# Block products for the down projection of a hybrid layer's second FFN

## The chip, the cores and the metric

One core of one Trainium2 chip runs the whole layer in one launch. The metric is the device time of that launch in microseconds (us). TensorE (PE in the profile) multiplies 128x128 blocks into PSUM, VectorE (DVE) and ScalarE (ACT) do the elementwise work, GpSimd (POOL) does some of it and issues transfers, SyncE (SP) issues transfers.

## The reference

The layer has three sub-layers, each with an RMSNorm before it and one after it: a SwiGLU feed-forward network (FFN), a mixer (a gated linear recurrence beside windowed attention), and a second FFN. There are 512 tokens, a model width of 1024 and an FFN width of 2816, that is 22 chunks of 128. All data is float32. The change lies in the second FFN:

```python
def swiglu(x, w_gu, w_down):
    gate, up = jnp.split(x @ w_gu, 2, axis=-1)
    return (jax.nn.silu(gate) * up) @ w_down
...
        x = x + 0.5 * rms_norm(swiglu(rms_norm(x, ffn2_pre_g[l]), ffn2_w_gu[l], ffn2_w_down[l]), ffn2_post_g[l])
```

## The kernel before

**Three terms for one product.** Each float32 operand is split into a high part, rounded to `float32r` by an ACT copy, and a low part, the difference, taken by DVE. A product of two blocks is three matmuls into one PSUM bank: high by high, high by low, low by high.

**Units of weights.** The class `Weights` keeps the order of all weight work. A raw tile of 1 MB comes from HBM on SP's queue into one of `NRAW` = 3 buffers. A unit is 128x1024 numbers of it: an optional sum of raw blocks on DVE (`pre`, L220), a cast to the high part on ACT (L171, L211), and the low part on DVE (L176, L215). `take()` hands the next unit to TensorE and brings the preparation up to four units beyond it (`AHEAD`). `later(n, ...)` puts a step n units later. So nothing is scheduled by a compiler: each engine runs its instructions in the order in which the program wrote them, and waits on semaphores.

**Gate and up product.** From chunk 6 on (chunk 4 in the first FFN), `quad` makes two chunks of the hidden layer by seven block products instead of eight: a unit is 24 matmuls of 128x256 into one of three banks A, D and B (names `ab`, `db`, `bb` in the second FFN, L676). Its end gives `u2` and `g1`, the hidden values of the first and of the second half of the tokens. `low_parts` splits them into high and low (L680 on ACT, L683 on DVE), in pieces of 128x256.

**Down product.** The 22 chunks of the second FFN go in five groups, `GROUPS2` = 0-6, 6-10, 10-14, 14-18 and 18-22. Group 0 uses plain products. Groups 1 to 3, here called the middle groups, run two quads and then, for each half `dh` of the output's columns, 4 chunks by 4 token blocks by three matmuls of 128x512 (`mm3_out`, L1425 to L1427, into four banks `yb`). The eight blocks of the running sum `yp_b`, 128x512 each, are kept in SBUF: ACT copies them there after group 0, DVE adds each middle group's banks to them (L1446). The last group adds its product, squares, scales by the norm, turns the residual stream `xT` back by transposes (`otp`, L1481), adds it and stores the result (L1488 to L1512). `xT`, eight tiles of 128x512, stays in SBUF from the start of the kernel.

Of the kernel before, what the change touches and what calls it, by code (L numbers as in the profile page):

```python
# [15 lines left out]
P = 128  # L16
T = 512
# [11 lines left out]
NT2K = 44  # L29
NW = 8  # L30
NWS = 6
NRAW = 3
CLASSIC1, CLASSIC2 = 4, 6
PUMPS = [(2, 1)] * 8 + [(1, 1), (1, 0), (4, 0)]
FILLS = {1: 4, 2: 5, 4: 5, 5: 5, 7: 5}
WARM = 6
# [12 lines left out]
class Weights:  # L49
# [18 lines left out]
    def load(self):  # L68
# [43 lines left out]
def tile_layer(ctx: ExitStack, tc: tile.TileContext, out: bass.AP, **ins: bass.AP):  # L112
# [6 lines left out]
    tmp = ctx.enter_context(tc.tile_pool(name="tmp", bufs=2))  # L119
    small = ctx.enter_context(tc.tile_pool(name="small", bufs=4))  # L120
    psum = ctx.enter_context(tc.tile_pool(name="psum", bufs=8, space=bass.MemoryType.PSUM))
    E = mybir.EngineType
    ctx.enter_context(tc.manual_schedule(engines={E.PE, E.DVE, E.Activation, E.Pool, E.SP}))

    ALL = slice(0, T)
    HALF = [slice(0, T // 2), slice(T // 2, T)]

    def bank(name):
# [12 lines left out]
    def load_raw(srcs, nk, w, name):  # L141
        raw = wpool.tile([P, nk * w], F32, tag="raw", name=f"raw_{name}", bufs=NRAW).rearrange("p (k c) -> p k c", k=nk)
        o = 0
        for src in srcs:
            n = src.shape[1]
            sync.dma_start(raw[:, :, o:o + n], src.rearrange("(k p) c -> p k c", p=P))
            o += n
        return raw

    class Deferred:  # L150
# [5 lines left out]
        def run(self):  # L156
            dve.tensor_sub(*self.args)
# [110 lines left out]
    def add_down(f, n, dh):  # L268

        r = W.raw(lambda: load_raw([ins["ffn2_w_down"][0, f * P:(f + n) * P, dh * T:(dh + 1) * T]], n, T, f"bd{f}{dh}"))  # L270
        for i in range(0, n, 2):
            add_unit(r, lambda raw, i=i: raw[:, i:i + 2, :], 2, T, f"bd{f + i}{dh}")

    for f0, f1 in GROUPS2:
        for f in range(f0, f1, 2):
            (add_gate_up if f < CLASSIC2 else add_quad)(w2, f, "b")
        if f1 < FC:
# [58 lines left out]
    def preload(func):  # L336
        act.activation(dummy, eps, func)
# [84 lines left out]
            return o  # L422


    xT = [big.tile([P, T], F32, name=f"xT{c}", tag=f"xT{c}") for c in range(KD)]

    def x_parts(name):
        return [(t2k(f"xh_{name}{c}", F32R), t2k(f"xl_{name}{c}", F32R)) for c in range(KD)]
# [7 lines left out]
    class Next:  # L436
# [14 lines left out]
        def low(self, c, h):  # L451
            x_low(self.xs[c], xT[c][:, HALF[h]], col(self.pre, c), HALF[h])

# [184 lines left out]
    class Hidden:  # L638
# [21 lines left out]
            dve.tensor_sub(hl, us, hh.bitcast(F32))  # L660
            self.hs[f] = (hh, hl)

        def quad(self, f, last, ahead):

            n = f"{self.name}{f}"
            l, r = HALF
            hs = [(t2k(f"hh{n}{j}", F32R), t2k(f"hl{n}{j}", F32R)) for j in range(2)]

            def seven(b, form, first, ahead=AHEAD):
                hi, lo = W.take(ahead)  # L670
                for j in range(2):
                    o, js = b[:, HALF[j]], slice(j * P, (j + 1) * P)
                    for k in range(4):
                        xh, xl = self.nxt.t[form, k]
                        for i, (w, x) in enumerate(((hi, xh), (hi, xl), (lo, xh))):
                            pe.matmul(o, w[:, k, js], x, start=first and i + j + k == 0, stop=k == 3 and i == 2, skip_group_check=True)  # L676

            def low_parts(x, h):
                for j in range(2):
                    act.copy(hs[j][0][:, HALF[h]], x[:, HALF[j]])  # L680
                for j in range(2):
                    hh, hl = hs[j]
                    dve.tensor_sub(hl[:, HALF[h]], x[:, HALF[j]], hh.bitcast(F32)[:, HALF[h]])  # L683

            def last_half():
                dve.tensor_mul(g1, g1, u4)

            A, D, B = (bank(f"{s}{n}") for s in "adb")
            p1, p7, u2, u4, g1 = (wt(f"{s}{n}") for s in ("p1", "p7", "u2", "u4", "g1"))
            seven(A, "b11", True)  # L690
            act.copy(p1, A)
            seven(D, "t3", True)
            act.copy(p7, D)
            seven(A, "t2", False)
            act.copy(u2, A)
            seven(B, "b21", True)
            dve.tensor_add(p1, p1, B)  # L697
            W.later(1, act.activation, p1, p1, AF.Silu)
            seven(A, "t1", False)
            act.copy(u4, A)  # L700
# [6 lines left out]
            act.activation(g1, A, AF.Silu)  # L707
# [6 lines left out]
            for j in range(2):  # L714
                self.hs[f + j] = hs[j]

        def classic(self, n, banks, extra, ahead=AHEAD):

# [32 lines left out]
        def chunks(self, f0, f1, ahead=AHEAD):  # L751
            for f in range(f0, f1, 2):
                self.quad(f, f == f1 - 2, ahead if f == f1 - 2 else AHEAD)
            return [self.hs.pop(f) for f in range(f0, f1)]


    n1 = Next("a", gain=lambda c: g1[:, c:c + 1])
# [668 lines left out]
        pe.matmul(ps, hh[:, blk], lo[:, k, cs], start=False, stop=False)  # L1426
        pe.matmul(ps, hl_[:, blk], hi[:, k, cs], start=False, stop=stop)  # L1427

    parts = {}
    for g, (f0, f1) in enumerate(GROUPS2[:-1]):  # L1430
        hs = hid.chunks(f0, f1) if g else hid.classic(f1, banks, {3: [(n2.sums, 0)], 3.5: [(n2.lows, 0)], 4.5: [(n2.sums, 1)], 5: [(n2.lows, 1)]}, AHEAD - 1)
        for dh in range(2):
            ybanks = [bank(f"yb{g}{dh}{tb}") for tb in range(NB)]
            for f in range(f0, f1):
                if f % 2 == 0:
                    w = W.take()
                for tb in range(NB):
                    mm3_out(ybanks[tb], hs[f - f0], tb, w, f % 2, ALL, f == f0, f == f1 - 1)
                if g == 0 and (dh, f) in ((0, 0), (0, 2), (1, 2), (1, 4)):
                    (n2.sums if f == 2 * dh else n2.lows)(2 + dh)  # L1440
            for tb in range(NB):
                if g == 0:
                    parts[tb, dh] = t2k(f"yp_b{tb}{dh}")
                    act.copy(parts[tb, dh], ybanks[tb])
                else:
                    dve.tensor_add(parts[tb, dh], ybanks[tb], parts[tb, dh])  # L1446
    f0, f1 = GROUPS2[-1]
    hs = hid.chunks(f0, f1, ahead=5)
    preload(AF.Sqrt)
    grow = [t2k(f"grow{dh}") for dh in range(2)]  # L1450
    for dh in range(2):
# [12 lines left out]
    for tb in range(NB):  # L1464
# [7 lines left out]
        tot = small.tile([P, 1], F32, tag="tot", name=f"tot_b{tb}")  # L1472
        for i, f in steps:
            dh, c0, c1 = pieces[i]
            if (i, f) == (1, f0):

                tp = []
                for h in range(2):
                    tp.append(bank(f"otp{tb}{h}"))
                    for c in range(4):  # L1480
                        pe.transpose(tp[h][:, c * P:(c + 1) * P], xT[4 * h + c][:, tb * P:(tb + 1) * P], ident)  # L1481
                if end:
                    tail = wt("tail")[:, :T // 2]
                    act.copy(tail, tp[1][:, :T // 2])
            mm3_out(banks[i][:, :c1 - c0], hs[f - f0], tb, weights(f, dh), f % 2, slice(c0, c1), f == f0, f == f1 - 1)
            if f == f1 - 1:
                y = parts[tb, dh][:, c0:c1]
                dve.tensor_add(y, banks[i][:, :c1 - c0], y)  # L1488
                act.activation(wt(f"ysq{tb}{i}")[:, :c1 - c0], y, AF.Square, accum_out=ss[:, i:i + 1])  # L1489
                if end and i == 2:  # L1490
                    dve.tensor_add(tot, ss[:, 0:1], ss[:, 1:2])
                    last = wt("last")[:, :c1 - c0]
                    dve.tensor_mul(last, y, grow[dh][:, c0:c1])
                else:
                    pool.tensor_mul(y, y, grow[dh][:, c0:c1])  # L1495
# [45 lines left out]
```

## Time and profile before

| | |
|---|---|
| median of 3 runs | 884.54 us (884.53 to 886.26) |
| the profiled execution: its own time | 886.26 us |
| the profiled execution: span in the trace | 884.6 us |
| one middle group, from its first quad product to the next group's (the chain of waits) | 62.10 us |
| data moved by DMA | 86.68 MB |

The span runs from the first to the last instruction of the trace; the execution's own time is 1.66 us longer. The columns of the profile's lines are explained where they are first used. A matmul's duration in a row covers its way through the pipeline, so matmuls overlap, and the time that one of many takes is read from when the next starts.

### The profile page before, as it was taken

To read this page: it belongs to the slowest core of one execution; us is meant where nothing else is said; L and a number is where in the kernel's file an instruction comes from. 1 tells how busy PE (TensorE), PEld (TensorE's weight loads), DVE (VectorE), ACT (ScalarE), POOL (GpSimd) and SP (SyncE) were. 2 spreads that over 40 slices of the span, in tenths; PEclk is the share of its full clock that TensorE was granted. 3 is DMA by queue.
4 is the path that set the end of the run, shared out by engine and by line. 5 is a ranking of instruction groups with operands and counts; after the bars stand their busy time and mean duration, and the time that the engine had idled before them with its cause. 6 is when DMAs were issued, how large, how long until landed. Compare 5 with 4: busy or idle time off the path is not lost.

```text
span 884.6 us, 14243 instructions
## 1 busy us (share of the span) xinstructions
PE 873.8 (99%) x5768; PEld 801.5 (91%) x5768; DVE 668.5 (76%) x993; ACT 459.5 (52%) x791; POOL 129.0 (15%) x117
## 2 busy tenths in 40 slices
PE   8999999999999999999999999999999999999997
PEld 8988999989989998998887899888998998998996
DVE  4979758778778864889999679588677677777754
ACT  6646534544535554457787346535463452552542
POOL 2010000000000015435463154210000000000013
PEclk9999999999999999999999999999999999999999
DMA  7242243152242253332301130224232241261212
GB/s 240 73 152 83 92 142 103 54 162 72 73 142 97 84 167 96 96 96 76 115 1 49 60 131 5 93 95 143 96 127 65 96 145 46 96 190 37 86 46 96
DMA packets 83553, 86.68 MB, mean 98 GB/s; under 512 B 3664, under 2 KB 75680, under 8 KB 83488
## 3 DMA queue, kind: packets, MB, share of 16 engines
q1 hardware_dynamic: 83312, 85.64, 30.2%
q8 instruction: 45, 0.74, 0.3%
q14 instruction: 20, 0.16, 0.1%
q10 hardware_dynamic: 144, 0.13, 0.0%
q0 software_dynamic: 32, 0.00, 0.0%
HBM read 83.67 MB, written 2.10 MB: 97 GB/s over the span
## 4 chain that ended last, share of the span: by engine, by line
PE 91%; DVE 5%; ACT 2%; issue 1%; DMA 1%; POOL 0%; SPq 0%; POOLq 0%; DVEq 0%; ACTq 0%
PE aa L676 12%; PE ab L676 10%; PE da L676 6%; PE db L676 5%; PE ya L361 4%; PE ya L362 4%; PE ya L363 4%; PE yb L1426 4%; PE yb L1427 4%; PE yb L1425 4%; PE ba L676 3%; PE bb L676 3%; PE a_first L841 1%; PE an L380 1%; PE mn L380 1%; PE mn L387 1%
## 5 line engine op out<-in xcount | busy, mean ns | idle before, releaser
L361 PE MATMUL ya<-hha,whi_ad 128*128 128x512 f32 x158 | 61.5, 389 | 0.0
L362 PE MATMUL ya<-hla,whi_ad 128*128 128x512 f32 x158 | 61.5, 389 | 0.0
L363 PE MATMUL ya<-hha,wlo_ad 128*128 128x512 f32 x158 | 61.5, 389 | 0.0
L1425 PE MATMUL yb<-whi_bd,hhb 128*128 128x512 f32 x144 | 56.1, 389 | 0.0
L1426 PE MATMUL yb<-wlo_bd,hhb 128*128 128x512 f32 x144 | 56.1, 389 | 0.0
L1427 PE MATMUL yb<-whi_bd,hlb 128*128 128x512 f32 x144 | 56.0, 389 | 0.0
L1495 POOL TENSOR_TENSOR yp_b<-yp_b,grow 128x512 f32<-128x512 f32 (+1 forms) x8 | 9.7, 1222 | 282.0 <-ACT ysq L1489 282.0
L942 POOL MEMSET bd_w_rg<- 128x512 f32 x1 | 0.5, 528 | 266.0 <-PE aa L676 266.0
L363 PEld LDWEIGHTS ya<-hha,wlo_ad 128*128 128x128 f32 x158 | 29.7, 188 | 6.2
L361 PEld LDWEIGHTS ya<-hha,whi_ad 128*128 128x128 f32 x158 | 29.7, 188 | 6.1
L362 PEld LDWEIGHTS ya<-hla,whi_ad 128*128 128x128 f32 x158 | 29.7, 188 | 6.0
L1427 PEld LDWEIGHTS yb<-whi_bd,hlb 128*128 128x128 f32 x144 | 27.0, 188 | 5.6
L1425 PEld LDWEIGHTS yb<-whi_bd,hhb 128*128 128x128 f32 x144 | 27.0, 188 | 5.6
L1426 PEld LDWEIGHTS yb<-wlo_bd,hhb 128*128 128x128 f32 x144 | 27.0, 188 | 5.5
L176 DVE TENSOR_TENSOR wlo_bd<-raw_bd,whi_bd 128x1024 fp32r<-128x1024 f32 x22 | 26.4, 1219 | 3.6 <-ACT whi_bd L171 3.6
L171 ACT CAST whi_bd<-raw_bd 128x1024 fp32r<-128x1024 f32 x22 | 22.9, 1049 | 5.1 <-PE bb L676 3.8
L1446 DVE TENSOR_TENSOR yp_b<-yb,yp_b 128x512 f32<-128x512 f32 x24 | 16.4, 692 | 11.6 <-PE yb L1427 11.6
L1000 DVE TENSOR_TENSOR yp_a<-ya,yp_a 128x512 f32<-128x512 f32 x24 | 16.4, 686 | 8.8 <-PE ya L363 8.8
L697 DVE TENSOR_TENSOR p1a<-p1a,ba 128x512 f32<-128x512 f32 x9 | 6.2, 688 | 21.7 <-PE ba L676 21.7
L697 DVE TENSOR_TENSOR p1b<-p1b,bb 128x512 f32<-128x512 f32 x8 | 5.5, 688 | 18.2 <-PE bb L676 18.2
L380 PE MATMUL an<-xh_mx,whi_xl 128*128 128x256 f32 x64 | 15.9, 289 | 0.0
L381 PE MATMUL an<-xh_mx,wlo_xl 128*128 128x256 f32 x64 | 15.5, 283 | 0.0
(1523 smaller groups left out, 3418.4 us busy)
## 6 DMA issues: line engine op xcount, KB each, us to landing
raw_bd<-in_ffn_w_down SPq DMA_DIRECT2D x10, 1024.0 KB, 6.8
xn<-in_x SPq DMA_DIRECT2D x8, 256.0 KB, 4.6
raw_q<-in_w_in SPq DMA_DIRECT2D x4, 512.0 KB, 3.8
out_dram<-yp_b SPq DMA_DIRECT2D x7, 256.0 KB, 2.0
first<-in_ffn_w_gu SPq DMA_DIRECT2D x4, 256.0 KB, 5.1
raw_second<-in_ffn_w_gu SPq DMA_DIRECT2D x2, 512.0 KB
raw_ag__104<-in_ffn_w_gu SPq DMA_DIRECT2D x1, 1024.0 KB
raw_au__286<-in_ffn_w_gu SPq DMA_DIRECT2D x1, 1024.0 KB, 5.8
```

What stands on the lines that cost most here:

```text
L171: act.copy(two(hi, x), x)
L176: low.tensor_sub(two(lo, x), x, two(hi.bitcast(F32), x))
L361: pe.matmul(ps, hi[:, k, :], xh, start=start, stop=False)
L362: pe.matmul(ps, hi[:, k, :], xl, start=False, stop=False)
L363: pe.matmul(ps, lo[:, k, :], xh, start=False, stop=stop)
L380: pe.matmul(ps[:, sl], hi[:, k, :], xh, start=k == 0, stop=False)
L676: pe.matmul(o, w[:, k, js], x, start=first and i + j + k == 0, stop=k == 3 and i == 2, skip_group_check=True)
L1000: dve.tensor_add(parts[c], b, parts[c])
L1425: pe.matmul(ps, hh[:, blk], hi[:, k, cs], start=start, stop=False)
L1426: pe.matmul(ps, hh[:, blk], lo[:, k, cs], start=False, stop=False)
L1427: pe.matmul(ps, hl_[:, blk], hi[:, k, cs], start=False, stop=stop)
L1446: dve.tensor_add(parts[tb, dh], ybanks[tb], parts[tb, dh])
```

## The change

**Seven products in the middle groups.** In groups 1 to 3 the down product is cut into blocks: the hidden values into token halves by chunk pairs (a11 and a12 for the first half of the tokens, a21 and a22 for the second), the weights into chunk pairs by column halves (b11, b12, b21, b22). Seven products of such blocks and of sums of blocks replace eight. A unit of them (`seven` in `seven_down`) is 2 banks by 2 chunks by 3 matmuls of 128x512, 12 in all.

- The weights' sums are five DVE instructions per group (`combine`), each made one unit ahead of the unit that uses it; there are seven units per group where there were four.
- The sums of hidden blocks (s1 to s4) are four DVE instructions per group. Each of the seven left operands is rounded whole (`high` on ACT, `low` on DVE, 128x512), in place of 16 pieces of 128x256 on each of the two engines.
- The seven products use four pairs of banks (A, B, Dd, E_). After the first product ACT copies A to B. After each of the other six products ACT copies the pair into two `stage` tiles, and POOL issues transfers that add them to the running sum, which now lies in HBM (`accum_op`): 14 transfers of 256 KB per group.

**The running sum and the residual stream in HBM.** After group 0, ACT copies the banks into `stage` tiles, with the sign turned for the second half of the columns, and POOL issues eight writes to HBM. POOL then writes `xT`, two tiles of 1 MB, to HBM. The two raw buffers that this frees (`xT` now lies in two of `NRAW` = 5) take weights in the middle groups. POOL issues the loads of the running sum before the last group, and those of `xT` after its quads in the program's order.

**All quads of both FFNs.** The product `b21` now adds to a copy of bank A: ACT copies A to B instead of to `p1`, and the SiLU reads B. The DVE addition at L697 is gone.

```diff
-NRAW = 3
+NRAW = 5
+SEVEN_DOWN = 6, 18
...
+        unit(b11, "p", combine(dve.tensor_add, b12, b12, b22))
+        unit(b12, "q")
+        unit(b21, "r", combine(dve.tensor_add, b12, b12, b11))
+        unit(b12, "s", combine(dve.tensor_sub, b11, b12, b22))
+        unit(b22, "t", combine(dve.tensor_add, b21, b12, b21))
+        unit(b21, "u")
+        unit(b11, "v")
...
+            a12, a22 = self.blocks[1, 0], x
+            s1, s2, s4 = (wt(f"{s}{self.name}{f}") for s in ("s1", "s2", "s4"))
+            dve.tensor_sub(s1, a22, a21)
+            dve.scalar_tensor_tensor(s2, s1, -1.0, a11, op0=ALU.mult, op1=ALU.subtract)
+            for name, y in (("a22", a22), ("s1", s1), ("s2", s2)):
+                W.later(1, self.high, name, y)
...
+            self.steps = [lambda: self.low("s2"), last_sum, lambda: self.low("s4"), lambda: self.low("a22")]
...
             seven(A, "b11", True)
-            act.copy(p1, A)
+            act.copy(B, A)
...
-            seven(B, "b21", True)
-            dve.tensor_add(p1, p1, B)
-            W.later(1, act.activation, p1, p1, AF.Silu)
+            seven(B, "b21", False)
+            W.later(1, act.activation, p1, B, AF.Silu)
...
+        def seven(banks, form, first, stop):
+            w = hi, lo = W.take()
+            hh, hl_ = forms[form]
+            for i in range(2):
+                for k in range(2):
+                    js = slice(k * (T // 2) + i * P, k * (T // 2) + (i + 1) * P)
+                    pe.matmul(banks[i], hh[:, js], hi[:, k, :], start=first and k == 0, stop=False, skip_group_check=True)
+                    pe.matmul(banks[i], hh[:, js], lo[:, k, :], start=False, stop=False, skip_group_check=True)
+                    pe.matmul(banks[i], hl_[:, js], hi[:, k, :], start=False, stop=k == 1, skip_group_check=True)
+
+        def to_parts(banks, *blocks):
+            for i in range(2):
+                st = t2k("stage")
+                act.copy(st, banks[i])
+                for tb, dh in blocks:
+                    pool.dma_start(parts[2 * tb + i, dh], st, accum_op=ALU.add)
+
+        for banks, form, blocks in ((A, "a11", []), (Dd, "s3", [(1, 1)]), (B, "a12", [(0, 0)]), (A, "s2", [(1, 0)]),
+                                    (E_, "s4", [(0, 1)]), (Dd, "a22", [(1, 0)]), (A, "s1", [(1, 1), (0, 1)])):
+            seven(banks, form, form in ("a11", "s3", "s4"), True)
+            if hid.steps:
+                hid.steps.pop(0)()
+            if form == "a11":
+                for i in range(2):
+                    act.copy(B[i], A[i])
+            else:
+                to_parts(banks, *blocks)
...
-                if g == 0:
-                    parts[tb, dh] = t2k(f"yp_b{tb}{dh}")
-                    act.copy(parts[tb, dh], ybanks[tb])
-                else:
-                    dve.tensor_add(parts[tb, dh], ybanks[tb], parts[tb, dh])
+                st = t2k("stage")
+                act.activation(st, ybanks[tb], AF.Copy, scale=-1.0 if dh else 1.0)
+                pool.dma_start(parts[tb, dh], st)
+        for x, h in zip(x_tiles, xT_hbm):
+            pool.dma_start(h, x)
...
+            parts[tb, dh] = t2k(f"yp_b{tb}{dh}")
+            pool.dma_start(parts[tb, dh], in_hbm[tb, dh])
     hs = hid.chunks(f0, f1, ahead=5)
+    x_tiles, xT[:] = stream()
+    for x, h in zip(x_tiles, xT_hbm):
+        pool.dma_start(x, h)
...
-            if (i, f) == (1, f0):
+            if (i, f) == (1, f1 - 1 if tb == 0 else f0):
...
-                dve.tensor_add(y, banks[i][:, :c1 - c0], y)
+                (dve.tensor_sub if dh else dve.tensor_add)(y, banks[i][:, :c1 - c0], y)
```

More of the change, by code (lines that the diff above doesn't have):

```diff
@@ L66, in unit, with load, load_one @@
         self.left[raw] += 1
-    def load(self):
+    def load(self, n=1):
+        for _ in range(n):
+            self.load_one()
+    def load_one(self):
         if self.loaded < len(self.raws):
@@ L121, in tile_layer @@
     psum = ctx.enter_context(tc.tile_pool(name="psum", bufs=8, space=bass.MemoryType.PSUM))
+    hbm = ctx.enter_context(tc.tile_pool(name="hbm", bufs=1, space=bass.MemoryType.DRAM))
     E = mybir.EngineType
@@ L126, in tile_layer @@
     HALF = [slice(0, T // 2), slice(T // 2, T)]
+    HALF_D = [slice(0, T), slice(T, D)]
     def bank(name):
@@ L272, in add_down, with add_seven_down, of, unit @@
             add_unit(r, lambda raw, i=i: raw[:, i:i + 2, :], 2, T, f"bd{f + i}{dh}")
+    def add_seven_down(f):
+        wd = ins["ffn2_w_down"]
+        rx, ry = (W.raw(lambda i=i: load_raw([wd[0, (f + k) * P:(f + k + 2) * P, HALF_D[i]] for k in (0, 2)], 2, D, f"b{'yx'[i]}d{f}_")) for i in (1, 0))
+        first, second = HALF_D
+        b11, b21, b12, b22 = (ry, first), (ry, second), (rx, first), (rx, second)
+        def of(block):
+            return W.tiles[block[0]][:, :, block[1]]
+        def unit(block, n, pre=None):
+            def cast(raw):
+                hi, lo = w_tiles(2, T, f"bd{n}{f}_")
+                act.copy(hi, of(block))
+                return hi, lo
+            def low(raw, hi, lo):
+                dve.tensor_sub(lo, of(block), hi.bitcast(F32))
+            W.unit(block[0], cast, low, pre)
+        def combine(fn, o, x, y):
+            def run():
+                assert max(o[0], x[0], y[0]) < W.loaded
+                fn(of(o), of(x), of(y))
+            return run
+        unit(b11, "p", combine(dve.tensor_add, b12, b12, b22))
[5 more added lines that the diff above has]
+        unit(b11, "v")
     for f0, f1 in GROUPS2:
@@ L276, in tile_layer @@
             (add_gate_up if f < CLASSIC2 else add_quad)(w2, f, "b")
-        if f1 < FC:
+        if SEVEN_DOWN[0] <= f0 < SEVEN_DOWN[1]:
+            add_seven_down(f0)
+        elif f1 < FC:
             for dh in range(2):
@@ L422, in spread, with stream @@
             return o
-    xT = [big.tile([P, T], F32, name=f"xT{c}", tag=f"xT{c}") for c in range(KD)]
+    def stream():
+        xs = [wpool.tile([P, 4 * T], F32, tag="raw", name=f"xT{i}", bufs=NRAW) for i in range(2)]
+        return xs, [x[:, c * T:(c + 1) * T] for x in xs for c in range(4)]
+    x_tiles, xT = stream()
+    xT_hbm = [hbm.tile([P, 4 * T], F32, name=f"xT_hbm{i}") for i in range(2)]
     def x_parts(name):
@@ L661, in split, with high, low, form @@
             self.hs[f] = (hh, hl)
-        def quad(self, f, last, ahead):
+        def high(self, name, x):
+            hh = t2k(f"hh{name}", F32R)
+            act.copy(hh, x)
+            self.forms[name] = hh, x
+        def low(self, name):
+            hh, x = self.forms[name]
+            hl = t2k(f"hl{name}", F32R)
+            dve.tensor_sub(hl, x, hh.bitcast(F32))
+            self.forms[name] = hh, hl
+        def form(self, name, x):
+            self.high(name, x)
+            self.low(name)
+        def seven_left(self, f, x, second):
+            self.blocks[second, 0] = x
+            self.form("a12" if second else "a11", x)
+        def seven_right(self, f, x, second):
+            self.blocks[second, 1] = x
+            a11, a21 = self.blocks[0, 0], self.blocks[0, 1]
+            if not second:
+                s3 = wt(f"s3{self.name}{f}")
+                dve.tensor_sub(s3, a11, a21)
+                self.form("s3", s3)
+                return
+            a12, a22 = self.blocks[1, 0], x
[4 more added lines that the diff above has]
+                W.later(1, self.high, name, y)
+            def last_sum():
+                dve.scalar_tensor_tensor(s4, s2, -1.0, a12, op0=ALU.mult, op1=ALU.subtract)
+                self.high("s4", s4)
+                self.low("s1")
+            self.steps = [lambda: self.low("s2"), last_sum, lambda: self.low("s4"), lambda: self.low("a22")]
+        def quad(self, f, last, ahead, seven_down=False):
             n = f"{self.name}{f}"
             l, r = HALF
-            hs = [(t2k(f"hh{n}{j}", F32R), t2k(f"hl{n}{j}", F32R)) for j in range(2)]
+            hs = None if seven_down else [(t2k(f"hh{n}{j}", F32R), t2k(f"hl{n}{j}", F32R)) for j in range(2)]
             def seven(b, form, first, ahead=AHEAD):
@@ L678, in low_parts @@
             def low_parts(x, h):
+                if seven_down:
+                    (self.seven_right if h else self.seven_left)(f, x, last)
+                    return
                 for j in range(2):
@@ L688, in quad @@
             A, D, B = (bank(f"{s}{n}") for s in "adb")
-            p1, p7, u2, u4, g1 = (wt(f"{s}{n}") for s in ("p1", "p7", "u2", "u4", "g1"))
+            p1, p7, u4 = (wt(f"{s}{n}") for s in ("p1", "p7", "u4"))
+            u2, g1 = ((t2k if seven_down else wt)(f"{s}{n}") for s in ("u2", "g1"))
             seven(A, "b11", True)
-            act.copy(p1, A)
+            act.copy(B, A)
             seven(D, "t3", True)
@@ L713, in quad @@
                 W.later(2, low_parts, g1, 1)
-            for j in range(2):
-                self.hs[f + j] = hs[j]
+            if not seven_down:
+                for j in range(2):
+                    self.hs[f + j] = hs[j]
         def classic(self, n, banks, extra, ahead=AHEAD):
@@ L754, in chunks, with seven_forms @@
             return [self.hs.pop(f) for f in range(f0, f1)]
+        def seven_forms(self, f):
+            self.forms, self.blocks = {}, {}
+            for i in (0, 1):
+                self.quad(f + 2 * i, i, AHEAD, True)
+            return self.forms
     n1 = Next("a", gain=lambda c: g1[:, c:c + 1])
@@ L1427, in mm3_out, with seven_down @@
         pe.matmul(ps, hl_[:, blk], hi[:, k, cs], start=False, stop=stop)
-    parts = {}
-    for g, (f0, f1) in enumerate(GROUPS2[:-1]):
-        hs = hid.chunks(f0, f1) if g else hid.classic(f1, banks, {3: [(n2.sums, 0)], 3.5: [(n2.lows, 0)], 4.5: [(n2.sums, 1)], 5: [(n2.lows, 1)]}, AHEAD - 1)
+    parts = {(tb, dh): hbm.tile([P, T], F32, name=f"yp_b{tb}{dh}") for tb in range(NB) for dh in range(2)}
+    def seven_down(f):
+        forms = hid.seven_forms(f)
+        A, B, Dd, E_ = ([bank(f"y{s}{f}{i}") for i in range(2)] for s in "abde")
+        def seven(banks, form, first, stop):
[23 more added lines that the diff above has]
+                to_parts(banks, *blocks)
+    for g, (f0, f1) in enumerate(GROUPS2[:-1]):
+        if g:
+            if g == 1:
+                W.later(4, W.load, 2)
+            seven_down(f0)
+            continue
+        hs = hid.classic(f1, banks, {3: [(n2.sums, 0)], 3.5: [(n2.lows, 0)], 4.5: [(n2.sums, 1)], 5: [(n2.lows, 1)]}, AHEAD - 1)
         for dh in range(2):
@@ L1441, in tile_layer @@
             for tb in range(NB):
-                if g == 0:
-                    parts[tb, dh] = t2k(f"yp_b{tb}{dh}")
-                    act.copy(parts[tb, dh], ybanks[tb])
-                else:
-                    dve.tensor_add(parts[tb, dh], ybanks[tb], parts[tb, dh])
-    f0, f1 = GROUPS2[-1]
+                st = t2k("stage")
[3 more added lines that the diff above has]
+            pool.dma_start(h, x)
+    f0, f1 = GROUPS2[-1]
+    in_hbm, parts = parts, {}
+    for tb in range(NB):
+        for dh in range(2):
+            parts[tb, dh] = t2k(f"yp_b{tb}{dh}")
+            pool.dma_start(parts[tb, dh], in_hbm[tb, dh])
     hs = hid.chunks(f0, f1, ahead=5)
+    x_tiles, xT[:] = stream()
+    for x, h in zip(x_tiles, xT_hbm):
+        pool.dma_start(x, h)
     preload(AF.Sqrt)
```

## The prediction

> **What bounds the kernel now.** I read the page first, then the waits of TensorE, then the chain of waits in the middle groups, then the busy time of each engine there, stage by stage.
>
> ```profile
> span 884.6 us, 14243 instructions
> PE 873.8 (99%) x5768; PEld 801.5 (91%) x5768; DVE 668.5 (76%) x993; ACT 459.5 (52%) x791; POOL 129.0 (15%) x117
> ...
> PE 91%; DVE 5%; ACT 2%; issue 1%; DMA 1%; POOL 0%; SPq 0%; POOLq 0%; DVEq 0%; ACTq 0%
> ```
> ```profile
> PE warm L828 <- POOL ident masks.py:199: 1.4, 1, 1.4
> PE rms_lru L406 <- DVE acc_lru L1358: 0.7, 1, 0.7
> ```
> ```profile
> core 0: us, PE busy (x) PEld busy (x) DVE busy (x) ACT busy (x) POOL busy (x), PEclk, DMA share, GB/s
> 626.19:688.29 62.10, 62.10 (x435) 58.34 (x434) 43.34 (x50) 28.15 (x39) 0.00 (x0) 1.00 0.32 103
> 688.29:750.39 62.10, 62.10 (x435) 58.34 (x434) 45.11 (x53) 27.68 (x38) 0.00 (x0) 1.00 0.33 102
> ```
>
> TensorE has no gap: 91% of the chain is its own, its two longest waits are 1.4 and 0.7 us, and in two middle groups it is busy 62.10 of 62.10 us at full clock. VectorE has 17 us to spare per group, ScalarE 34, POOL does nothing and the DMA engines stand at a third. So matmuls taken away there shorten the time one for one, as long as what replaces them fits into these spares and comes in time.
>
> **The gain: 36 matmuls.** The chain of waits gives the time of one matmul:
>
> ```profile
> 663.63 2.88 PE ab L676 x24
> 666.51 0.23 PE yb L1425
> ...
> 688.29 2.87 PE ab L676 x24
> ```
>
> The down product of a middle group runs from 666.51 to 688.29, 21.78 us for 4 chunks x 8 blocks x 3 = 96 matmuls: 0.227 us each. After the change a group has 7 x 2 x 2 x 3 = 84 of the same shape: 12 fewer, 2.72 us. Three groups: 36 x 0.227 = 8.17 us. A group becomes 59.4 us, one unit of the down product 2.72 us.
>
> **VectorE.** The rows that go and the rows that price what comes:
>
> ```profile
> L1446 DVE TENSOR_TENSOR yp_b<-yb,yp_b 128x512 f32<-128x512 f32 x24 | 16.4, 692 | 11.6 <-PE yb L1427 11.6
> L176 DVE TENSOR_TENSOR wlo_bd<-raw_bd,whi_bd 128x1024 fp32r<-128x1024 f32 x22 | 26.4, 1219 | 3.6 <-ACT whi_bd L171 3.6
> ```
> ```profile
> L683 DVE TENSOR_TENSOR hlb<-g1b,hhb 128x256 fp32r<-128x256 f32 x4 | 1.5, 419 | 0.5 <-ACT hhb L680 0.5
> ...
> L697 DVE TENSOR_TENSOR p1b<-p1b,bb 128x512 f32<-128x512 f32 x2 | 1.4, 688 | 4.6 <-PE bb L676 4.6
> ```
>
> Per group go 8 additions x 0.692 = 5.5, 16 small low parts x 0.419 = 6.7 and 2 of L697 = 1.4 us. There come 5 weight sums and 3 more weight low parts at 1.219 = 9.8, and 7 low parts and 4 sums of hidden blocks, 11 x 0.69 = 7.6 us. 45.1 - 13.6 + 17.4 = 48.9 of 59.4 us: 82%, not the bound by itself.
>
> **ScalarE.**
>
> ```profile
> L171 ACT CAST whi_bd<-raw_bd 128x1024 fp32r<-128x1024 f32 x4 | 4.2, 1052 | 1.3 <-PE bb L676 1.3
> L680 ACT CAST hhb<-g1b 128x256 fp32r<-128x256 f32 x4 | 1.4, 405 | 1.1 <-DVE g1b L686 1.1
> ...
> L700 ACT COPY u4b<-ab 128x512 f32<-128x512 f32 x2 | 1.2, 577 | 1.4 <-PE ab L676 1.4
> ```
>
> 16 x 0.405 = 6.5 us go; 3 casts x 1.052, 7 high parts and 14 copies of a bank at about 0.58 come, 15.3 us: 27.7 + 8.8 = 36.5 of 59.4 us. The new copy of A to B costs what the copy to `p1` did; removing L697 is worth nothing in time, since TensorE never waited for it.
>
> **The join.** Totals do not say that each operand is in time. The tightest place is the end of a group's second quad, since the last hidden block only exists then. Call that moment 0 (666.51 above). The rows there:
>
> ```profile
> 658.51 2.35 DVE L176 TENSOR_TENSOR wlo_bd<-raw_bd,whi_bd 128x1024 fp32r<-128x1024 f32 x2
> ...
> 664.99 1.22 DVE L176 TENSOR_TENSOR wlo_bd<-raw_bd,whi_bd 128x1024 fp32r<-128x1024 f32 x1
> 666.13 0.75 DVE L683 TENSOR_TENSOR hlb<-u2b,hhb 128x256 fp32r<-128x256 f32 x2
> 667.17 0.69 DVE L686 TENSOR_TENSOR g1b<-g1b,u4b 128x512 f32<-128x512 f32 x1 [0.29 <-ACT g1b L707]
> ```
> ```profile
> 666.54 0.60 ACT L707 ACTIVATE g1b<-ab 128x512 f32<-128x512 f32 x1 [0.72 <-PE ab L676]
> ```
> ```profile
> 594.26 0.68 DVE L500 TENSOR_TENSOR t13l_f<-ta_f,t13h_f 128x512 fp32r<-128x512 f32 x1
> 594.87 0.68 DVE L500 TENSOR_TENSOR t24l_f<-tb_f,t24h_f 128x512 fp32r<-128x512 f32 x1
> ```
>
> Back to back, a 128x1024 costs VectorE 1.14 (two in 2.35) and a 128x512 0.61 us (594.26 to 594.87). In the changed program VectorE's queue from -1.52 on (664.99) holds: a weight low part, a weight sum, the low part of a12 (done at 1.4), g1 x u4, s1, s2 (3.2), a weight low part, the low part of s2 (5.0), weight, s4, the low part of s1, weight, the low part of s4 (9.1), weight, sum, the low part of a22 (11.9). TensorE starts a12 at 5.4, s2 at 8.2, s4 at 10.9, a22 at 13.6 and s1 at 16.3. The spares are 4.0, 3.2, 1.8 and 1.7 us; a handover between engines costs 0.29 us in the row of L686, three of them take 0.9 us of the last. ScalarE must have copied A to B by 5.4: silu (0.6), a weight cast that waits for the sum at 0.8 (1.8), the high parts of a22, s1 and s2 (3.9), then the copies, at 4.5 and 5.1; the second is needed at 6.8. Spare 0.9 us. So I count nothing for the join and bound it by 1 us per group: with all handovers at double cost the last spare is exceeded by 0.1 us, and one more of 0.9 us fits under the bound. No gain is possible here, as TensorE is full.
>
> **The transfers.** No row of before shows an adding transfer, nor a large one from POOL. The nearest:
>
> ```profile
> q1 hardware_dynamic: 83312, 85.64, 30.2%
> ...
> raw_bd<-in_ffn_w_down SPq DMA_DIRECT2D x10, 1024.0 KB, 6.8
> ...
> out_dram<-yp_b SPq DMA_DIRECT2D x7, 256.0 KB, 2.0
> ```
> ```profile
> L322 POOL DMA_DIRECT2D g1rows<-in_ffn_pre_g x1: 715/715/715, 1.5 to 1.5; - x1
> ...
> DMA to landing us min/median/max: 4.5/4.5/4.5
> ```
>
> Occupation: 85.64 MB took 30.2% of the span, 267 us, 3.1 us per MB, 0.8 us for 256 KB. An addition also reads its target; I take twice, 1.6 us, between 0.8 and the 4.5 us of POOL's one transfer as a serial price. In a group 14 x 1.6 = 23 us join the weights' 0.33 x 62.1 = 20.5: 43 of 59.4 us, hidden. The Trainium skill, page "Collectives: The Full Stack", section "The bandwidth ceiling", says that an adding transfer runs at about half the rate of a copy because of its second read; by it the price is the 1.6 us again, but only for transfers between cores, and no trace here shows it.
>
> Latency: who waits? ScalarE's copies into `stage` tiles reuse a tile whose transfer must have landed; behind such a copy stand the next weight casts and the next quad's copy of A to B. The last of them, for the second bank of s1, waits for the first transfer of a12. That is the third of its group, issued about 10 us after the join, and ScalarE reaches the next quad's copy in time (24.8) if it has landed by 22.6: 12 us for three transfers, against 2.0 and 4.5 us of the rows. POOL's queue also waits for the earlier addition to the same block, at least a unit before; behind it stand only further transfers. SP's loads into the two freed buffers wait for the two writes of `xT`, issued by POOL behind eight writes at the first quad's start; their weights are cast in the second quad, over 20 us later, against 6.8 us for 1 MB. Running sum and `xT` come back under the last group's quads, 40.31 us long; if either were late, each us would count in full. The moved transposes are the same work.
>
> **Sum.** Against the profiled execution: 886.26 - 8.17 = 878.1 us, with a span of 876.4. Its own time is 1.72 us above the median; against the median: 884.54 - 8.17 = 876.4 us, 0.92% faster. About 0.2% (1.8 us) is what a measurement of this kernel can tell from no change.
>
> **Rivals.** *B, late at the join:* TensorE waits once or twice per group because VectorE or ScalarE comes later than worked out, for instance held by POOL's issues. For: VectorE rises to 82% and one spare is 0.9 us. Against: every spare is positive. At the bound of 1 us per group: 879.4 us; at 2 us, 882.4.
>
> *C, slower: the adding transfers fill the DMA engines.* The group then takes 20.5 + 14 a us, a being one transfer's occupation. It decides from a = 2.8 us (59.4); from 3.0 us on (62.1) the whole gain is lost. At four times the copy's price, a = 3.3, the group takes 66.7 us, 7.3 more than forecast: 876.4 + 3 x 7.3 = 898 us. For: 42 transfers with a read, an addition and a write to HBM, of a kind that no row shows. Against: it needs over three times the copy's price in every row that moves 256 KB or more.
>
> *D, nothing gained:* the products saved and the waits added cancel, 883 to 886 us; the instruction order shows the 36 matmuls gone, so this needs 2.7 us of waits per group by chance.
>
> **Chances.** Forecast (876.4, give or take 0.5) 0.63, B 0.13, D 0.04, C 0.20. Faster 0.76, same 0.04, slower 0.20. The range goes from 875.4 (1 us of scatter below) over B and D to 886.0; C lies outside.
>
> **What would show it.** Right: the next quad of each middle group starts 59.4 us after the last one's, TensorE is busy in all of it, the seven products take 2.72 us each, VectorE is at 49 us per group, and the transfers land within 10 us. B: waits of TensorE for `hl` or `hh` tiles or for a copied bank just behind a quad. C: a DMA share near 1 in the middle groups and waits for `stage` or for raw tiles. The forecast is wrong if a middle group takes over 60.5 us or if the last group waits for its loads.

## The result and the profile after

The changed kernel takes 879.43 us (median of 4 runs, 879.18 to 880.96) against 884.67 us before (4 runs); the ratio is 0.994, 95% interval 0.9923 to 0.9958. It is faster by 5.2 us where 8.2 were forecast. The profiled execution took 880.96 us with a span of 879.2, against 886.26 and 884.6. The profiled executions reach the first middle group at 624.3 to 626.3 us, and those with the same work from there on agree within about 0.2 us up to SP's drain at the end, so stages and tails are compared below as distances within a trace.

The page of the changed kernel, its first rows, its chain and its transfers (the last column of a transfer is the median time from issue to landing in us):

```profile
span 879.2 us, 14431 instructions
PE 866.2 (99%) x5732; PEld 795.2 (90%) x5732; DVE 680.0 (77%) x982; ACT 491.3 (56%) x839; POOL 176.0 (20%) x179
...
q1 hardware_dynamic: 83408, 85.64, 30.8%
q0 software_dynamic: 7936, 19.41, 9.5%
...
PE 91%; DVE 5%; ACT 1%; issue 1%; DMA 1%; POOL 0%; SPq 0%; POOLq 0%; DVEq 0%; ACTq 0%
...
yp_b<-stage POOLq DMA_DIRECT2D x50, 256.0 KB, 8.2
...
xT<-xT_hbm POOLq DMA_DIRECT2D x2, 1024.0 KB, 8.1
```

TensorE has 5732 matmuls where it had 5768, 36 fewer, and its share of the chain is still 91%. The busy time of the engines by stage, in the three middle groups, the quads of the last group and the rest, and the longest waits of TensorE (us in total, times, longest):

```profile
core 0: us, PE busy (x) PEld busy (x) DVE busy (x) ACT busy (x) POOL busy (x), PEclk, DMA share, GB/s
626.07:685.45 59.38, 59.38 (x423) 56.08 (x422) 47.33 (x50) 36.85 (x52) 9.17 (x13) 1.00 0.68 213
685.45:744.83 59.38, 59.38 (x423) 56.09 (x422) 50.67 (x53) 38.54 (x55) 12.14 (x15) 1.00 0.70 169
744.83:804.21 59.38, 59.38 (x423) 56.08 (x422) 50.69 (x53) 38.58 (x55) 12.15 (x15) 1.00 0.70 170
804.21:844.52 40.31, 40.31 (x338) 40.31 (x337) 29.85 (x33) 23.21 (x34) 10.73 (x17) 1.00 0.77 209
844.52:879.20 34.68, 25.50 (x141) 21.75 (x139) 14.50 (x32) 10.72 (x29) 10.44 (x9) 0.90 0.16 61
```
```profile
PE warm L935 <- POOL ident masks.py:199: 1.4, 1, 1.4
PE rms_lru L451 <- DVE acc_lru L1465: 0.7, 1, 0.7
```

A middle group takes 59.38 us and TensorE is busy in all of it; the longest waits are the two of before. The last group's quads take the same 40.31 us, and no wait for the running sum or for `xT` shows. So the 8.17 us are won up to there, and 2.9 of them must be lost behind.

The end of the program shows where. First the instructions at its last line in the kernel before, then in the changed kernel (min/median/max duration in ns, then the first and the last start in us):

```profile
L1537 POOLq DRAIN  x3: 45/102/910, 880.7 to 884.3; - x3
L1537 SPq DRAIN  x3: 7/7/7, 883.7 to 884.0; - x3
...
L1537 PEldq DRAIN  x2: 13/1179/2345, 876.0 to 884.1; - x2
```
```profile
L1691 POOLq EVENT_SEMAPHORE  x4: 17/17/17, 878.5 to 879.1; - x4
L1691 POOLq DRAIN  x3: 51/93/5991, 872.4 to 878.9; - x3
L1691 SPq DRAIN  x3: 7/7/7, 875.6 to 878.7; - x3
...
L1691 PEldq DRAIN  x2: 13/1179/2345, 867.7 to 878.8; - x2
```

POOL's last work, first in the kernel before, then in the changed kernel (start, duration in us):

```profile
880.76 0.72 POOL L1509 TENSOR_TENSOR yp_b<-yp_b,tail 128x256 f32<-128x256 f32 x1 [1.74 <-ACT yp_b L1508]
```
```profile
872.48 0.73 POOL L1663 TENSOR_TENSOR yp_b<-yp_b,tail 128x256 f32<-128x256 f32 x1 [1.74 <-ACT yp_b L1662]
```

Each engine ends with a drain, and then all meet at a barrier. TensorE comes to its drain at 867.7 in place of 876.0, 8.3 us earlier, and SP, which waits for the last output's landing, at 875.6 in place of 883.7, 8.1 us earlier. But POOL's first drain takes 5.99 us in place of 0.91. It begins beside POOL's last addition (872.48) and ends at 878.4, and POOL's next instruction starts at 878.5. Before, the span ended 0.9 us after SP's drain (883.7 to 884.6); by that the span here would be 875.6 + 0.9 = 876.5 us. It is 879.2: 2.7 us are POOL's.

### The profile page after: what moved, and what is told of

It reads as the page before. It is cut to its first block, busy times and chain, and to the rows that moved or that the text cites. A ratio compares the mean times of both kernels' runs of the same rounds, so it can differ in the third digit from the quotient of the medians.

```text
span 879.2 us, 14431 instructions
## 1 busy us (share of the span) xinstructions
PE 866.2 (99%) x5732; PEld 795.2 (90%) x5732; DVE 680.0 (77%) x982; ACT 491.3 (56%) x839; POOL 176.0 (20%) x179
## 4 chain that ended last, share of the span: by engine, by line
PE 91%; DVE 5%; ACT 1%; issue 1%; DMA 1%; POOL 0%; SPq 0%; POOLq 0%; DVEq 0%; ACTq 0%
PE aa L772 12%; PE ab L772 10%; PE da L772 6%; PE db L772 5%; PE ya L408 4%; PE ya L406 4%; PE ya L407 4%; PE ba L772 3%; PE bb L772 3%; PE a_first L948 2%; PE yb L1533 1%; PE yb L1532 1%; PE yb L1534 1%; PE ya L1549 1%; PE ya L1550 1%; PE ya L1551 1%
## 5 line engine op out<-in xcount | busy, mean ns | idle before, releaser
L1558 POOL DMA_DIRECT2D yp_b<-stage x42 | 36.5, 1146 | 147.2 <-ACT stage L1556 138.1
L1532 PE MATMUL yb<-whi_bd,hhb 128*128 128x512 f32 x48 | 18.7, 389 | 0.0
L1533 PE MATMUL yb<-wlo_bd,hhb 128*128 128x512 f32 x48 | 18.7, 389 | 0.0
L1534 PE MATMUL yb<-whi_bd,hlb 128*128 128x512 f32 x48 | 18.7, 389 | 0.0
L578 POOL TENSOR_TENSOR acca_r<-acca_r,sq_r 128x512 f32<-128x512 f32 x6 | 8.4, 1406 | 48.1 <-ACT sq_r L437 48.1
L183 DVE TENSOR_TENSOR wlo_bd<-raw_bd,whi_bd 128x1024 fp32r<-128x1024 f32 x10 | 12.1, 1222 | 7.0 <-ACT whi_bd L178 7.0
L705 POOL TENSOR_TENSOR usb<-usb,gsb 128x512 f32<-128x512 f32 x5 | 7.6, 1537 | 33.0 <-DVE usb L702 21.8
L406 PE MATMUL gt<-xh_mx,whi_gt 128*128 128x512 f32 x32 | 14.2, 443 | 0.0
L1532 PE MATMUL ybl<-whi_bd,hhb 128*128 128x512 f32 (+1 forms) x36 | 13.5, 375 | 0.0
L1533 PE MATMUL ybl<-wlo_bd,hhb 128*128 128x512 f32 (+1 forms) x36 | 13.2, 366 | 0.0
```

The source lines that it names most:

```text
L406: pe.matmul(ps, hi[:, k, :], xh, start=start, stop=False)
L1532: pe.matmul(ps, hh[:, blk], hi[:, k, cs], start=start, stop=False)
L1558: pool.dma_start(parts[2 * tb + i, dh], st, accum_op=ALU.add)
```

## Experiments

**Theory 1:** POOL's drain has grown because of the 62 transfers that POOL now issues (42 adding ones, 8 writes and 8 loads of the running sum, 2 writes and 2 loads of `xT`) beside the one that it issued before, and it stands in the way because POOL works until 873.2. **Theory 2:** the drain waits for something at the end itself. **Theory 3:** the writes to HBM make the last output land later.

**e1: POOL without work in the last token block.**

```diff
-                    pool.tensor_mul(y, y, grow[dh][:, c0:c1])
+                    (dve if end else pool).tensor_mul(y, y, grow[dh][:, c0:c1])
...
-                pool.tensor_add(y, y, tail)
+                dve.tensor_add(y, y, tail)
```

In the last block the three outputs are also scaled in another order, so that this addition comes last on VectorE.

> The changed kernel, with POOL's three elementwise steps of the last token block on VectorE, so that POOL's last instruction before its drain ends at about 866.5 us instead of 873.2. Theory 1 (POOL's drain at the program's end has become 5.99 us long because of the 62 transfers that POOL issued, and it starts when POOL's last step is done): the drain still takes about 6 us but ends at about 872.5, before the last output has landed, so the span falls by about 2.5 us to 876.5 to 877.0 and the time to about 876.7 us, 0.9% below the kernel before. Theory 2 (the drain waits for something at the end itself, such as the last output's write to HBM, whatever POOL did before): the drain still ends at about 878.5 and the time stays at 879.2 to 879.6 us. Theory 3 (the last output lands later because of the traffic to HBM): the time stays also, and SP's wait for the landing stands at the end of the chain.

Measured: 877.59 us (877.18 to 877.79, 5 runs), ratio to before 0.9916 (0.9903 to 0.993). The drain at the end:

```profile
L1691 POOLq DRAIN  x3: 51/93/6554, 863.5 to 875.3; - x3
L1691 SPq DRAIN  x3: 7/7/7, 874.8 to 875.1; - x3
```

The drain begins beside a 1.29 us product in place of the 0.73 us addition; beyond that it takes 5.26 us in both kernels. But it starts at 863.5 and is over at 870.1, 4.7 us before SP comes, and the span ends with SP again. So theory 3 falls, the drain did not wait for the last output either (against theory 2), and most of the loss comes back. The time is 0.9 us above the expectation: with VectorE's longer list in the last block, 8.7 us pass from TensorE's drain to SP's (866.1 to 874.8) in place of 7.9.

**e2: an early drain.** One instruction behind POOL's last transfer:

```diff
         pool.dma_start(x, h)
+    pool.drain()
     preload(AF.Sqrt)
```

> The changed kernel, with one more drain instruction on POOL, behind its last transfer (the second load of the residual stream) and ahead of its elementwise steps in the last group, where POOL has over 20 us to spare. Theory 1a (what the drain has to clear has piled up with the transfers and is cleared once): the early drain takes 5 us or more, the one at the end falls back to 0.9 us or less, and the time falls by 2.5 us to about 876.7 us. Theory 1b (a drain is long in any program that issued so many transfers, each time anew) and theory 2 (it waits for the end's own work): the one at the end stays near 6 us and the time at 879.2 to 879.6 us.

Measured: 876.85 us (876.58 to 878.39, 4 runs), ratio to before 0.9912 (0.9899 to 0.9926).

```profile
L1603 POOLq DRAIN  x1: 10833/10833/10833, 827.9 to 827.9; - x1
```
```profile
L1692 POOLq DRAIN  x3: 39/98/832, 872.7 to 876.4; - x3
L1692 SPq DRAIN  x3: 7/7/13, 875.8 to 876.1; - x3
```

The drain at the end falls from 5.99 to 0.83 us, although POOL ends its work as late as in the changed kernel, and the span again ends 0.9 us after SP's drain. What is cleared has piled up and is cleared once (theory 1a); theory 2 falls. The loss is back: 884.76 - 876.85 = 7.9 us of the 8.17. None of its runs is as long as the shortest of the changed kernel (879.18).

**e3, e4, e7, e8: POOL's transfers alone, in the kernel before.** 60 times a block of `xT` to a spare block in HBM, one after the other; then only one row of it, 60, 20 and 120 times:

```diff
+    spare = hbm.tile([P, T], F32, name="spare")
+    for _ in range(60):
+        pool.dma_start(spare, xT[0])
     f0, f1 = GROUPS2[-1]
     hs = hid.chunks(f0, f1, ahead=5)
```

> The kernel before, with 60 further transfers of 256 KB issued by POOL, one after the other, from a block of the residual stream to a spare block of HBM that nobody reads. Theory 1: POOL's first drain at the end grows from 0.91 us to about 6 us, as in the changed kernel, and the span by about 2 us (the drain would start at about 881.5 and end at 886.6 to 887.5; before, the last landing ends the span at 884.6): 886.5 to 888 us of span. Theory 2 and 3: the drain stays at about 0.9 us and the span at 884.6, give or take 0.5.

> The same 60 further transfers from POOL in the kernel before, but each of one row of 2 KB in place of 128 rows (60 packets in all in place of 7680). If the drain grows by the transfer (about 0.085 us each), it takes about 6 us again and the span is 886.5 to 888 us; if it grows by the packet or by the byte (5.1 us for some 7900 packets), it stays below 1.1 us and the span at 884.6, give or take 0.5. Theories 2 and 3 expect the latter as well, but have then failed in the run with whole blocks.

> The kernel before with 20 further transfers of one row of 2 KB from POOL, in place of the 60 of e4. If the drain grows in proportion to their number: 0.91 + 20 x 0.082 = 2.6 us for the first drain, and no change of the span, since the last landing then still comes later. If it is one fixed price of any program that issues such transfers: 5.8 us again. If it grows by steps or only beyond some number: 0.9 us.

> The same with 120 transfers of one row. In proportion to the number: 0.91 + 120 x 0.082 = 10.7 us for the first drain, and a span 4.9 us above that of e4. If what is cleared has a limit that 60 transfers have reached: 5.8 us again, and e4's span.

Measured, single runs: 887.21, 887.90, 884.56 and 910.31 us, with spans of 885.5, 886.2, 882.8 and 908.6. POOL's drain in each, in the order e3, e4, e7, e8, and SP's in the first three:

```profile
L1541 POOLq DRAIN  x3: 51/102/5822, 878.9 to 885.2; - x3
L1541 SPq DRAIN  x3: 7/7/7, 882.0 to 885.0; - x3
```
```profile
L1541 POOLq DRAIN  x3: 40/102/5832, 879.5 to 885.9; - x3
L1541 SPq DRAIN  x3: 7/7/7, 882.7 to 885.6; - x3
```
```profile
L1541 POOLq DRAIN  x3: 40/102/2565, 878.8 to 882.6; - x3
L1541 SPq DRAIN  x3: 7/7/7, 882.0 to 882.3; - x3
```
```profile
L1541 POOLq DRAIN  x3: 40/102/10733, 897.1 to 908.3; - x3
```

60 transfers of 256 KB and 60 of 2 KB cost the same, 5.82 and 5.83 us: the price goes by the transfer, not by the byte. (In packets the two differ as well, though less than I had expected: the software queue counts 4832 and 1952.) And it is linear: from 20 to 60 transfers 3.27 us more, from 60 to 120 4.90 us more, 0.082 us each both times. With it the changed kernel's drain is 0.91 + 62 x 0.082 = 6.0 us; it has 5.99. These executions came to their tail earlier than the profiled one of before, so their spans lie below the expected ones; counted from SP's first drain, the span ends 3.5 us later in e3 and e4 (882.0 to 885.5, 882.7 to 886.2) and 0.8 us in e7, against 0.9 before: the longer drain costs 2.6 us with 60 transfers and nothing with 20, as expected. The span of e8 is another matter: it was to be 4.9 us above e4's and is 22.4 above. The transfers go one at a time, about 1.8 us apart, so POOL was still issuing at 878.8 and came late to its products, for which VectorE waited:

```profile
POOL spare L1450 <- DMA spare<-xT: 235.6, 119, 5.4
...
DVE yp_b L1515 <- POOL yp_b L1499: 21.5, 2, 21.0
```

That is the placing of the experiment and not the drain.

**e5: the rival of the DMA engines, at its point of decision.** On top of e2, each adding transfer is issued twice, and so is each of the eight writes after group 0:

```diff
+                    pool.dma_start(spare[2 * tb + i, dh], st, accum_op=ALU.add)
...
+                pool.dma_start(spare[tb, dh], st)
```

> The changed kernel with the early drain of e2, and each adding transfer issued a second time, to eight spare blocks of HBM that nobody reads (28 in a middle group in place of 14). It puts the rival C (the adding transfers fill the DMA engines) at its point of decision: worked out with the occupation that the changed kernel's trace gives, 34.3% of 59.38 us for the 14 of a group, 1.45 us each, the group's transfers occupy 20.5 + 28 x 1.45 = 61 us, as 14 transfers of 2.9 us each would. If the engines' occupation sets the end: a middle group takes 61 to 64 us, the DMA share goes to 0.95 or more, TensorE waits for operands behind stage or raw tiles, and the time is 882 to 891 us. If the occupation overlaps (a share near 1 is no limit yet): groups of 59.4 us, a share of 0.95 or more, and 877 us. If latency decides and not occupation: groups over 62 us at a share below 0.9.

Measured: 883.48 us (single run). Its stages, TensorE's longest wait, and POOL's issue of the loads of `xT`:

```profile
684.26:743.64 59.38, 59.38 (x423) 56.09 (x422) 50.89 (x52) 37.73 (x54) 23.73 (x28) 1.00 1.03 230
743.64:803.02 59.38, 59.38 (x423) 56.09 (x422) 50.93 (x53) 39.52 (x56) 24.40 (x29) 1.00 1.02 231
803.02:843.33 40.31, 40.31 (x338) 40.31 (x337) 29.99 (x33) 23.60 (x35) 20.79 (x28) 1.00 1.10 236
843.33:881.80 38.47, 28.38 (x141) 23.51 (x139) 14.81 (x32) 10.61 (x29) 10.37 (x9) 0.86 0.33 125
```
```profile
PE otp L1640 <- DMA xT<-xT_hbm: 3.5, 2, 1.8
```
```profile
841.87 1.11 POOL L1606 DMA_DIRECT2D xT<-xT_hbm  x2 [0.20 <-issue]
```

Two neighbouring matmuls behind those waits (start, duration in us):

```profile
853.55 0.63 PE L1533 MATMUL ybl<-wlo_bd,hhb 128*128 128x512 f32 x1
853.98 0.63 PE L1534 MATMUL ybl<-whi_bd,hlb 128*128 128x512 f32 x1
```

The same two loads in the changed kernel:

```profile
L1602 POOL DMA_DIRECT2D xT<-xT_hbm x2: 543/543/543, 824.4 to 827.8; - x2
```

With the DMA share at 1.03 the middle groups still take 59.38 us, so none of the three readings holds whole. The group does not become longer, as the second said, but the time is not 877 us: the transfers run behind, POOL's loads of the running sum wait for the additions ahead of them, the loads that follow are issued late (`xT` at 841.9 us, in the changed kernel at 824.4), and TensorE waits 3.5 us for `xT` in the last group. The rest of the 6.6 us over e2 lies in the same stage, which takes 38.47 us where e2 has 31.99. TensorE's granted clock falls to 0.50 during these waits and is back at about 857.4: the ten matmuls of 128x512 that start from 852.98 on, 0.43 us apart where the trace has 0.23 otherwise, take 2.1 us longer. A share near 1 was paid where the next needed data was queued, not where it arose. A mean busy share above 1 can only come about where times are added up that overlap, so it does not say that the engines were full, and no run here shows where they would be.

**e6: VectorE later at the join.** On top of e2, the subtraction for s1 is done five times in place of once:

```diff
+            for _ in range(4):
+                dve.tensor_sub(s1, a22, a21)
             dve.tensor_sub(s1, a22, a21)
```

> The changed kernel with the early drain of e2, and the VectorE subtraction that makes s1 done five times in place of once (the same result each time): 4 x 0.61 = 2.4 us more on VectorE at the join of each middle group, from 49 to 51.4 of 59.4 us in all. If the spare is what the prediction worked out (0.9 us for the copies of A to B, behind the high part of s2 on ScalarE; 0.6 us in the changed kernel's trace), TensorE waits 1.5 to 1.8 us for such a copy at the start of a12, no other operand is late, a middle group takes 60.9 to 61.2 us, and the time is 881.4 to 882.3 us. If what counts is only the engine's total (VectorE still below 87%), the group stays at 59.4 us and the time at 877 us.

Measured: 884.28 us (single run), 7.4 above e2. TensorE's longest wait, a group and the added instructions:

```profile
PE yb L1551 <- ACT yb L1569: 6.4, 3, 2.1
```
```profile
686.39:748.23 61.84, 59.72 (x423) 56.01 (x422) 52.63 (x56) 37.73 (x54) 11.27 (x14) 1.00 0.67 161
```
```profile
728.79 2.87 DVE L747 TENSOR_TENSOR s1b<-g1b,g1b 128x512 f32<-128x512 f32 x4
731.69 0.69 DVE L748 TENSOR_TENSOR s1b<-g1b,g1b 128x512 f32<-128x512 f32 x1
```

The wait is the one named, once in each of three groups, and no other came. It is longer than expected (2.1 us) because subtractions into the same tile do not follow at 0.61 us but at 0.73: the delay is 2.9 us, less a spare of 0.8. VectorE's total went up by 2 us with 9 to spare, and the group became 2.5 us longer: the total decides nothing here, the order at the join does.

**e9: the change of the quads alone**, in the kernel before:

```diff
-            act.copy(p1, A)
+            act.copy(B, A)
...
-            seven(B, "b21", True)
-            dve.tensor_add(p1, p1, B)
-            W.later(1, act.activation, p1, p1, AF.Silu)
+            seven(B, "b21", False)
+            W.later(1, act.activation, p1, B, AF.Silu)
```

> The kernel before with one part of the change alone: in all quads ScalarE copies bank A to bank B in place of p1, the product b21 adds to that copy, and VectorE's addition at L697 is gone. The prediction counts nothing for it, because TensorE never waited for that addition: the time stays within 0.2% of the kernel before, and a middle group at 62.10 us. The other reading, that the copy into the bank now stands between two products and TensorE waits for it: 0.3 us or more in each of the 17 quads, 5 us or more in all, with waits of TensorE for bank B.

Measured: 884.86 us (11 runs) against 885.03, ratio 1.0 (0.9991 to 1.0009), and quads that begin 62.10 us apart (641.69 and 703.79 in the chain of waits). This part is worth nothing, as forecast.

**e10: the early drain put later.**

```diff
+    late = small.tile([P, 1], F32, tag="late", name="late")
+    pool.tensor_mul(late, hs[-1][0][:, :1].bitcast(F32), hs[-1][0][:, :1].bitcast(F32))
+    pool.drain()
```

> The changed kernel with the early drain of e2 put later: POOL first squares one column of the last hidden chunk's high part (nobody reads the result), which exists at about 843 us, and then drains, some 7 us after its last transfer has landed. The early drain of e2 took 10.83 us where 62 transfers x 0.082 give 5.1 on top of the 0.2 us of a drain without them. If the rest was that the last loads were still in flight: 5 to 5.5 us now. If an early drain is longer in itself: about 10.8 us again, and POOL's first product of the last group comes up to 5 us late, which the path to the end does not feel by more than 1 us. In both cases the drain at the end stays at 0.9 us, and the time at 876.6 to 877.6 us.

Measured: 877.38 us (876.72 to 878.23, 4 runs), ratio 0.9912 (0.9898 to 0.9925), the same as e2.

```profile
L1605 POOLq DRAIN  x1: 5626/5626/5626, 842.5 to 842.5; - x1
```
```profile
842.49 0.36 POOL L1604 TENSOR_TENSOR late<-hhb 128x1 f32<-128x1 f32 x1 [15.60 <-ACT hhb L779]
848.24 1.28 POOL L1652 TENSOR_TENSOR yp_b<-yp_b,grow 128x512 f32<-128x512 f32 x1 [5.38 <-ACT ysq L1646]
```

Less the 0.36 us of the product beside which it begins, the drain takes 5.27 us: 62 transfers' worth, as at the end of the changed kernel and in e1. The other 5 us of e2's early drain are gone when the last loads have landed. The early drains of e6 and e5 also began right behind the last loads and took 10.61 and 14.34 us, for 62 and 112 transfers, again some 5 us above the price by the transfer. That fits a drain that waits for transfers in flight, but no run shows what it waits for.

## Why the prediction was right, and where it was wrong

That the kernel becomes faster, and by which mechanism, was right, and the time lies within the range; the likeliest time was 3.0 us too low. That the range held is luck: it went up to 886.0 us for the sake of rivals B and D, and 879.43 us is by chance the 879.4 us of B at 1 us per group, while no group was longer than the forecast 59.4 us. The loss came from a place that neither the forecast nor a rival named.

- **36 matmuls, 8.17 us: right.** The group takes 59.38 us, as forecast, and up to TensorE's drain 8.3 us are won.
- **VectorE and ScalarE: slightly low, without effect.** VectorE has 50.7 us per group (48.9 worked out), ScalarE 38.6 (36.5). TensorE waits for neither.
- **The join: right.** The spare of 0.9 us for the copies of A to B is 0.8 us by e6 (2.9 - 2.1), and where it was used up, the wait fell on that copy, the mechanism of rival B. The other spares of the list were not used up in any run.
- **The transfers.** In the group from 685.45 to 744.83 the software queue has 34.3% of the DMA engines' time, 15 issues begin in it, and a group has 14 transfers:

```profile
q1 hardware_dynamic: 5312, 6.29, 34.9%
q0 software_dynamic: 2014, 3.67, 34.3%
...
yp_b<-stage POOLq DMA_DIRECT2D x15, 256.0 KB, 9.0
```

  That is 20.4 us, 1.45 us for each of 14, close to the 1.6 us taken. The Trainium skill ("Collectives: The Full Stack", section "The bandwidth ceiling") has the adding phase of a collective between cores at about half the rate of the copying one. For these transfers within one core, 1.45 us against the prediction's 0.8 us for a copy comes near to that. "The transfers land within 10 us" was too tight: the median is 9.0 us in that group, and single ones take up to 13.4 us, without a wait of TensorE. Rival C was priced by a rule that e5 does not bear out: at the occupation that was to decide, the groups did not grow, and 6.6 us in all came due in the last group.
- **The step that failed: the sum.** "886.26 - 8.17 = 878.1" took it that whatever TensorE wins reaches the end. The prediction followed POOL's queue through the middle groups only ("behind it stand only further transfers") and had no term for the end of the program. The missing term is POOL's drain: 62 x 0.082 = 5.1 us longer, of which SP's wait for the last output covers a part, and 2.7 us stand out. With the drain hidden (e2) the forecast of 876.4 us is met within 0.5 us.

The trace of before held a faint sign of it and no price. POOL's drain took 0.91 us there, of which 0.72 lie beside its last addition, and POOL had issued one transfer; SP, which issues all the weights' transfers, has drains of 7 ns. The Trainium skill ("VectorE: DVE Perf Modes", section "The DRAIN you can't avoid") gives the drains that the runtime adds ahead of and behind a program as about 12 ns, constant, on all five engines. The drains here stand at the last line of the program itself, and no run shows whether that sentence means them: SP's take 7 ns, but POOL's first 0.83 to 10.73 us and TensorE's 2.35 us.

## What to carry over

When an engine gets a new kind of work, follow it to the last instruction of the program: a transfer issued by POOL was charged 0.082 us at the next drain, whatever its size, and a drain put into POOL's idle time took 2.6 us off the changed kernel (879.43 to 876.85). Engine totals and a DMA share of 1 say little by themselves: the groups kept their length at a share of 1.03, and grew by 2.5 us when one engine with 9 us to spare came 2.9 us late at the one place where another waited.

## What the runs showed of the hardware

- POOL's drain at the end: 0.91, 2.57, 5.83 and 10.73 us for 1, 21, 61 and 121 transfers issued by POOL, in each case with about 0.7 us beside POOL's last addition. It is paid once: behind an early drain, the one at the end takes 0.83 us.
- An early drain with the last loads still in flight took 10.83 us, against 5.3 us for the same number of landed transfers.
- The DMA share can stand at 1.02 to 1.10 for over 150 us without a wait of TensorE, while POOL's issues slip behind.
- The granted clock fell to 0.50 when TensorE waited for `xT` in e5, and for over 4 us behind the wait matmuls of 128x512 started 0.43 us apart in place of 0.23.
